# A two-layer hybrid trunk on one core: sliding-window queries kept as [feature, token], their rotation done through memory from GpSimd's queue

## The chip, the cores and the metric

One Trainium2 chip; the kernel runs on 1 of its cores. The metric is device time in microseconds. A core has five engines with queues of their own: PE (TensorE; PEld is its weight load), DVE (VectorE), ACT (ScalarE), POOL (GpSimd) and SP (SyncE, which here issues the transfers).

## The reference, cut to what matters

512 tokens, model width 1024, two layers, float32. Each layer normalises its input, makes one combined projection, runs two branches on it (a gated delta rule with 8 heads, and sliding-window attention with 16 query heads and 2 key/value heads), merges them by gates, projects, and then runs an MLP.

```python
h = rmsnorm(x, pre_mix_g)
proj = h @ w_in        # dn q k v z | beta | decay | sw q | sw k | sw v | gate a | gate b
q = partial_rope(q_in.reshape(B, S, 16, 64), positions)   # rotates the first 16 of 64
k = partial_rope(k_in.reshape(B, S, 2, 64), positions)
scores = einsum(q_block, k_window) * 64 ** -0.5           # window 128, blocks of 128
m = max(max(scores), sink)
probs = exp(scores - m) / (sum(exp(scores - m)) + exp(sink - m))
o = probs @ v
mix = (sigmoid(gate_a) * (dn_out @ w_up_dn) + sigmoid(gate_b) * (o @ w_up_sw)) @ w_o
x = x + rmsnorm(mix, post_mix_g)
x = x + rmsnorm(relu(rmsnorm(x, pre_mlp_g) @ w_ff1) ** 2 @ w_ff2, post_mlp_g)
```

## The kernel before, in words

**Matmuls.** Every large product is three matmuls in a rounded 32-bit format: weights and activations are split into a high and a low part, and high x high, high x low and low x high are summed. Weights come in chunks of 128 x 1024 (512 KB) in the order that `chunk_order` lists. SP loads a chunk, ScalarE copies its high part (`wh`, L319), VectorE subtracts the low part (`wl`, L320), four chunks ahead of use (`LOOK`). There are two forms. In a "unit" (`mm_a`, L335 to L337) the weights stand still and 512 tokens stream: the result is [128 features, 512 tokens], 24 matmuls of 512 columns. `mm_a2` (L346 to L348) is half a unit, 256 tokens. In the other form (`mm_b`, L355 to L357; `mm_b4`, L382 to L384) a tile of 128 tokens stands still and weight columns stream: the result is [128 tokens, columns].

**The norm and its transposes.** The input is [token, feature]; `norm_turn` transposes a token tile on TensorE (`ps_n`, L455) and splits it (ACT L459, DVE L461). In the first layer this is mixed with the first projection by a fixed order. At the layers' turn, `last_tiles` makes the four token tiles of the MLP's last product; the next layer's input tiles 0 and 1 are transposed inside it, tiles 2 and 3 (L555, L558) inside the next layer's first projection.

**The projection of attention queries, keys, values, beta and decay** (1296 columns) is of the second form, in three column blocks of 432 (`NB`): block 0 at L511 to L545 or L551 to L558, blocks 1 and 2 at L655 to L659. `evac_b` copies them to `qt[t]` (queries of a token tile, [token, feature]), `kv[t]` and `ba` (beta and decay). From `ba` a chain of small operations (L605 to L625) leads to a prefix sum on TensorE (`ps_g`, L627) and its transposition (`ps_gt`, L636). This is stored to memory (`gd`), and eight decay masks D are loaded back, cut by GpSimd (L647), raised to powers by ScalarE and stored (`dd`).

**Attention groups between units.** `MIX` (L46) lists 16 steps: which units run (K: a delta-rule key, `ps_kp`; G: gate b, `ps_gb`; A: gate a, `ps_ga`), and after each step's units one attention group (token tile t, key head g, parity e). The first group of a tile rotates queries and keys on GpSimd (`att_rope`, L780 to L785), transposes keys (`ps_k`, L801); each pair of groups transposes four 128 x 128 blocks of queries (`ps_q`, L814), which ScalarE and VectorE scale and split into `qT` (L819, L820). Then come the scores (`ps_s`, L846 and L847), softmax on VectorE and ScalarE (M, L849 to L870), its transposes (`ps_pt`, L876) and the product with the values (`ps_o`, L892), added back into `qt`. After all groups the output is split for the next product (`oT`, L1118 to L1124, 32 pieces of 128 x 128 a layer).

**What sets the order.** The code states the work; a scheduler places each engine's instructions in its queue, free to interleave work that doesn't depend on each other, and keeps to the stated order only inside the `Order` blocks. Each queue then runs strictly in its order.

## Time and profile before

| what | value |
|---|---|
| time, median of 3 runs | 1878.31 us (1876.77 to 1879.1) |
| profiled execution, its own time | 1874.57 us |
| its span, first to last instruction | 1872.9 us |
| mean granted TensorE clock | 0.999 |
| DMA, share of 16 engines, and rate | 42.0% (SP's queue), 136 GB/s |

The profile is of one execution. Its views name an instruction by engine, line, and `out<-in`, the tiles that it writes and reads, with buffer numbers left out. A group's row has its count, then busy time and the mean of one in ns, then idle time of the engine before it and what ended that. A row of the time-ordered view has its start and its length in us, and in brackets the idle time before it. The length of a matmul is modelled and overlaps the next one's, so the distance between starts tells the pace. A row of the windows has a stretch, its length, and the busy time of each engine in it.

### The profile page before, as it was taken

To read this page: it belongs to the slowest core of one execution; us is meant where nothing else is said; L and a number is where in the kernel's file an instruction comes from. 1 tells how busy PE (TensorE), PEld (TensorE's weight loads), DVE (VectorE), ACT (ScalarE), POOL (GpSimd) and SP (SyncE) were. 2 spreads that over 40 slices of the span, in tenths; PEclk is the share of its full clock that TensorE was granted. 3 is DMA by queue.
4 is the path that set the end of the run, shared out by engine and by line. 5 is a ranking of instruction groups with operands and counts; after the bars stand their busy time and mean duration, and the time that the engine had idled before them with its cause. 6 is when DMAs were issued, how large, how long until landed. Compare 5 with 4: busy or idle time off the path is not lost. (4 is left out here: it accounts for less than half of the span.)

```text
span 1872.9 us, 26807 instructions
## 1 busy us (share of the span) xinstructions
PE 1847.6 (99%) x9716; PEld 1534.1 (82%) x9716; DVE 1281.5 (68%) x2466; ACT 939.7 (50%) x1913; POOL 208.1 (11%) x385
## 2 busy tenths in 40 slices
PE   8999999999999999999999999999999999999998
PEld 7888788888888888888888887888888888888886
DVE  5499795777656667684556997857775667586834
ACT  6678732344434645454356887233333346454442
POOL 1322102121100000000012221022111000000000
PEclk9999999999999999999999999999999999999999
DMA  5633436333363253544245333553433533534631
GB/s 179 202 115 117 120 125 196 102 119 109 86 215 127 91 188 97 176 168 170 83 143 188 103 126 105 160 173 102 125 97 110 194 124 99 183 114 158 205 119 45
DMA packets 123445, 255.40 MB, mean 136 GB/s; under 512 B 32609, under 2 KB 49313, under 8 KB 123314
## 3 DMA queue, kind: packets, MB, share of 16 engines
q1 hardware_dynamic: 123314, 253.71, 42.0%
q8 instruction: 76, 1.25, 0.3%
q14 instruction: 55, 0.45, 0.1%
HBM read 224.70 MB, written 28.97 MB: 135 GB/s over the span
## 5 line engine op out<-in xcount | busy, mean ns | idle before, releaser
L320 DVE TENSOR_TENSOR wl<-wr,wh 128x1024 fp32r<-128x1024 f32 (+1 forms) x332 | 402.6, 1222 | 331.2 <-ACT wh L319 323.4
L319 ACT CAST wh<-wr 128x1024 fp32r<-128x1024 f32 (+1 forms) x332 | 344.1, 1041 | 561.8 <-PE ps_f L336 145.9
L335 PE MATMUL ps_f<-g_h,wh 128*128 128x512 f32 x448 | 174.3, 389 | 0.0
L336 PE MATMUL ps_f<-g_l,wh 128*128 128x512 f32 x448 | 174.3, 389 | 0.0
L337 PE MATMUL ps_f<-g_h,wl 128*128 128x512 f32 x448 | 174.3, 389 | 0.0
L397 PE MATMUL ps_p<-wl,P_h 128*128 128x512 f32 x336 | 131.2, 391 | 0.8 <-DVE wl L320 0.8
L399 PE MATMUL ps_p<-wh,P_l 128*128 128x512 f32 x336 | 130.8, 389 | 0.0
L395 PE MATMUL ps_p<-wh,P_h 128*128 128x512 f32 x336 | 129.5, 389 | 0.0
L434 POOL TENSOR_TENSOR pr<-pq,pw 128x1 f32<-128x1 f32 x16 | 9.3, 583 | 809.5 <-DVE pq L433 809.5
L336 PEld LDWEIGHTS ps_f<-g_l,wh 128*128 128x128 f32 x448 | 84.1, 188 | 17.5
L335 PEld LDWEIGHTS ps_f<-g_h,wh 128*128 128x128 f32 x448 | 84.1, 188 | 17.4
L337 PEld LDWEIGHTS ps_f<-g_h,wl 128*128 128x128 f32 x448 | 84.1, 188 | 17.4
L397 PEld LDWEIGHTS ps_p<-wl,P_h 128*128 128x128 f32 x336 | 63.1, 188 | 15.6 <-DVE wl L320 2.3
L395 PEld LDWEIGHTS ps_p<-wh,P_h 128*128 128x128 f32 x336 | 63.1, 188 | 13.3 <-ACT wh L319 0.2
L399 PEld LDWEIGHTS ps_p<-wh,P_l 128*128 128x128 f32 x336 | 63.1, 188 | 12.8
L382 PE MATMUL ps_b<-wh,h_h 128*128 128x432 f32 (+1 forms) x192 | 71.1, 371 | 0.0
L383 PE MATMUL ps_b<-wl,h_h 128*128 128x432 f32 (+1 forms) x192 | 70.4, 367 | 0.0
L384 PE MATMUL ps_b<-wh,h_l 128*128 128x432 f32 (+1 forms) x192 | 70.0, 366 | 0.0
L285 DVE TENSOR_TENSOR wr<-wr 128x1024 f32<-128x1024 f32 x48 | 58.0, 1221 | 2.4 <-DMA wr<-in_weights_dram 1.9
L335 PE MATMUL ps_qp<-h_h,wh 128*128 128x512 f32 x128 | 54.9, 429 | 0.0
L336 PE MATMUL ps_qp<-h_l,wh 128*128 128x512 f32 x128 | 54.1, 423 | 0.0
L864 ACT ACTIVATE M<-M,nm 128x128 f32<-128x128 f32 x128 | 49.8, 391 | 5.9 <-DVE nm L859 5.9
(356 smaller groups left out, 4855.4 us busy)
## 6 DMA issues: line engine op xcount, KB each, us to landing
wr<-in_weights_dram SPq DMA_DIRECT2D x308, 512.0 KB
wr<-in_weights_dram SPq DMA_DIRECT2D x24, 432.0 KB
D<-dd SPq DMA_DIRECT2D x32, 256.0 KB
xd<-xo SPq DMA_DIRECT2D x12, 512.0 KB
xt<-xd SPq DMA_DIRECT2D x24, 256.0 KB
D<-gd SPq DMA_DIRECT2D x16, 256.0 KB
dd<-D SPq DMA_DIRECT2D x16, 256.0 KB
kkd<-kk SPq DMA_DIRECT2D x16, 256.0 KB
```

What stands on the lines that cost most here:

```text
L285: tt(out=a, in0=a, in1=o, op=ALU.add)
L319: nc.scalar.copy(wh[:, :w], wr[:, :w])
L320: sub(out=wl[:, :w], in0=wr[:, :w], in1=wh[:, :w].bitcast(F32), op=ALU.subtract)
L335: mm(ps, lhsT=wh[:, k, :], rhs=hi, start=k == 0, stop=False)
L336: mm(ps, lhsT=wh[:, k, :], rhs=lo, start=False, stop=False)
L337: mm(ps, lhsT=wl[:, k, :], rhs=hi, start=False, stop=k == KT - 1)
L382: mm(pss[t], lhsT=hi[:, tsl], rhs=wh[:, r, :], start=k == 0, stop=False)
L383: mm(pss[t], lhsT=hi[:, tsl], rhs=wl[:, r, :], start=False, stop=False)
L384: mm(pss[t], lhsT=lo[:, tsl], rhs=wh[:, r, :], start=False, stop=k == KT - 1)
L395: mm(pss[t], lhsT=hi[:, c], rhs=wh[:, r, :], start=first, stop=False, skip_group_check=onto)
L397: mm(pss[t], lhsT=hi[:, c], rhs=wl[:, r, :], start=False, stop=False, skip_group_check=onto)
L399: mm(pss[t], lhsT=lo[:, c], rhs=wh[:, r, :], start=False, stop=last, skip_group_check=onto)
```

## The change

Queries are made by eight units of the first form (Q units, `ps_q`), so that they leave the projection as [feature, token] in `q8[g]` and need no transposes. The 272 columns that are left (beta, decay, keys, values) are one block of the second form, in three chunks of 3, 3 and 2 rows. The weights' columns are packed so that the four heads of a unit's rows that rotate stand together.

The rotation of queries needs rows of one head beside their partner rows. It goes through memory: four transfers out of `q8[g]` (`qd`), three in (`rq`), two multiplications and an addition on VectorE with tables of cosine and sine in [feature, token] form, one transfer out (`qrd`) and four back. All twelve are issued from GpSimd's queue. The tables are made once, behind the second Q unit of the first layer, by 16 small copies on ScalarE and eight transposes on TensorE, and kept in memory.

In the first layer, Q unit 0 runs in two token halves around the projection of the last token tile. At the layers' turn, four Q units run in token halves (`halves`, the code that the MLP's first units had), with the transposes of input tiles 2 and 3 inside; the 272-column block follows. The remaining four Q units are in `MIX`, which is listed anew, and the groups come in another order: (0,0), (1,0), (0,1), (1,1) and so on, by tile and key head. A group's preparation (keys' rotation and transposition, `qT`) is stated one group ahead. The decay masks are in a function `decays`, called between Q units 2 and 3 in the first layer. The attention output replaces the queries in `q8`, and is split in pieces of 512 columns. Buffers of 4 KB a partition (`X4`, six) become buffers of 8 KB (`X8`, three).

```diff
-NB = 432
+NB = 272
-MIX = "G K K G K K G K K G K K G GA GA GA".split()
+MIX = "QQ KQ QK G KG KG G KG K GK GK G A A A A".split()
-NA2 = NA + 2
+NA2 = NA + 1
...
+    def halves(aT, name, turn):
+        us = []
+        for i in range(4):
+            us.append(((PZ, PZ, PM, PM)[i](name), weights()))
+            if i != 2:
+                mm_a2(us[i][0], aT, 0, us[i][1])
+                continue
+            for j in range(2):
+                mm_a2(us[i][0], aT, 0, us[i][1], range(j * 4, j * 4 + 4))
+                turn(2 + j)
+        for ps, w in us:
+            mm_a2(ps, aT, 1, w)
+        return [ps for ps, w in us]
...
+        def q_rope(g):
+            spots = [(q8[g][e * HD + a * HALF:e * HD + (a + 1) * HALF].rearrange("p (m n) -> p m n", m=4),
+                      lambda d, a=a, e=e: d[g, a].rearrange("(m e) i n -> e i m n", e=2)[e])
+                     for e in range(2) for a in range(2)]
+            for a, d in spots:
+                pdma(d(qd), a)
+            r_, rs_ = T[2]("rq"), T[3]("rq")
+            flat = lambda d: d.rearrange("a b i n -> (a b i) n")
+            pdma(r_, flat(qd[g]))
+            for a in range(2):
+                pdma(rs_[a * 64:(a + 1) * 64], qd[g, 1 - a].rearrange("b i n -> (b i) n"))
+            tt(out=r_, in0=r_, in1=tables[0][0], op=ALU.mult)
+            tt(out=rs_, in0=rs_, in1=tables[0][1], op=ALU.mult)
+            tt(out=r_, in0=r_, in1=rs_, op=ALU.add)
+            pdma(flat(qrd[g]), r_)
+            for a, d in spots:
+                pdma(a, d(qrd))
+        def q_unit(m, ps=None):
+            if ps is None:
+                ps = PM("ps_q")
+                mm_a(ps, hT)
+            nc.scalar.copy(q8[m // 4][:, m % 4 * 512:(m % 4 + 1) * 512], ps)
+            if m % 4 == 3:
+                q_rope(m // 4)
...
-            ws = [weights() for _ in range(4)]
+            q_tables()
+            ps_q = halves(hT, "ps_q", lambda t: norm_turn(xs_next[t], t, nxt[1]))
+            order.end()
+            for m, ps in enumerate(ps_q):
+                q_unit(m, ps)
+            ws = [weights() for _ in range(3)]
+            pb0 = four(0)
+            for j, w in enumerate(ws):
+                for t in range(NT):
+                    mm_b(pb0[t][:, :NB], ws, hT, t, range(3 * j, min(3 * j + 3, KT)), 3)
...
         def att_q(t, g):
-            ps = PS("ps_q")
-            for i in range(4):
-                j = g * 4 + i
-                tr(ps[:, i * P:(i + 1) * P], qt[t][:, j * P:(j + 1) * P], ident)
+            q_ = c4(q8[g])[:, :, t * P:(t + 1) * P]
...
+        if l == 0:
+            q_unit(0, ps_q0)
+            q_unit(1)
+            rotary()
+            q_tables()
+            q_unit(2)
+            decays()
+            q_unit(3)
+        else:
+            decays()
+        def att_ready(i):
+            if i + 1 < 16 and groups[i + 1][1:] == (0, 0):
+                att_rope(groups[i + 1][0])
+            if i < 16:
+                t, g, e = groups[i]
+                if (g, e) == (0, 0):
+                    att_keys(t)
+                if e == 0:
+                    att_q(t, g)
+        def o_split(g):
+            for i in range(4):
+                oT.append(pair(T[i], "oT"))
+                split(q8[g][:, i * 512:(i + 1) * 512], *oT[-1])
```

Three places in the queues. First GpSimd's in the first layer, from the cut of the decay masks (D) on; `qt` and `kv` are queries and keys of a token tile, `cs` the cosine and sine, `rt` a scratch tile. Before:

```order
L647 AFFINE_SELECT D<-D 128x512 x8
L780 TENSOR_TENSOR rt<-qt_409,cs 128x128
L781 TENSOR_TENSOR rt<-qt_409,cs 128x128
L782 TENSOR_TENSOR rt<-qt_409,cs 128x128
L783 TENSOR_TENSOR rt<-qt_409,cs 128x128
L784 TENSOR_TENSOR qt_409<-rt 128x16x8
L785 TENSOR_TENSOR qt_409<-rt 128x16x8
```

Now, with `q_116` the first half of the queries and `ub` a tile of the delta rule's solver:

```order
L735 AFFINE_SELECT D<-D 128x512 x4
L570 DMA qd<-q_116 8x4x512
L735 AFFINE_SELECT D<-D 128x512 x3
L570 DMA qd<-q_116 8x4x512
L735 AFFINE_SELECT D<-D 128x512
L570 DMA qd<-q_116 8x4x512 x2
L575 DMA rq<-qd 64x512
L821 MEMSET ub 128x1024
L822 MEMSET ub 128x32
L573 DMA rq<-qd 128x512
L575 DMA rq<-qd 64x512
L579 DMA qrd<-rq 128x512
```

The masks were one block, followed by the rotation of queries; now the transfers of the rotation stand between the masks, and no arithmetic on queries is left on GpSimd. Second, the same queue in the second layer, now:

```order
L570 DMA qd<-q_9080 8x4x512 x4
L575 DMA rq<-qd 64x512
L859 TENSOR_TENSOR rt<-kv,cs 128x16
L860 TENSOR_TENSOR rt<-kv,cs 128x16
L861 TENSOR_TENSOR rt<-kv,cs 128x16
L862 TENSOR_TENSOR rt<-kv,cs 128x16
L863 TENSOR_TENSOR kv<-rt 128x2x8
L864 TENSOR_TENSOR kv<-rt 128x2x8
L573 DMA rq<-qd 128x512
L575 DMA rq<-qd 64x512
```

The rotation of the first key tile came to stand between the loads of the queries' rows. Third, TensorE at the layers' turn, around the transposes of input tile 3 (`ps_n`). Before:

```order
L357 MATMUL ps_b<-wh,h_l 128x432
L455 MATMUL ps_n<-ident,xs 128x128 x8
L355 MATMUL ps_b<-wh,h_h 128x432
L356 MATMUL ps_b<-wl,h_h 128x432
L357 MATMUL ps_b<-wh,h_l 128x432
```

Now:

```order
L385 MATMUL ps_q<-h_h,wl 128x256
L506 MATMUL ps_n<-ident,xs 128x128 x8
L383 MATMUL ps_q<-h_h,wh 128x256
L384 MATMUL ps_q<-h_l,wh 128x256
L385 MATMUL ps_q<-h_h,wl 128x256
```

The matmuls around the transposes were those of the 432-column block, with a token tile standing still; now they are halves of Q units.

More of the change, by code (lines that the diff above doesn't have):

```diff
@@ L245, in rotary @@
         act(out=cs[:, :, 0, :], in_=ang, func=AF.Sin, bias=hp, scale=-1.0)
+        for c in range(2):
+            ct = T[6 + c]("ct")
+            cv = ct.rearrange("p (t a b i) -> p t a b i", t=NT, a=2, i=HALF)
+            for a in range(2):
+                for t in range(NT):
+                    src = cs[:, t, c, :].unsqueeze(1).broadcast_to([P, 8, HALF])
+                    act(out=cv[:, t, a], in_=src, func=AF.Copy, scale=-1.0 if c > a else 1.0)
+            ps = PS("ps_cs")
+            for t in range(NT):
+                tr(ps[:, t * P:(t + 1) * P], ct[:, t * P:(t + 1) * P], ident)
+            ctT = T[6 + c]("ctT")
+            nc.scalar.copy(ctT, ps)
+            dma(csd[c], ctT)
     xd = dr.tile([S, D], F32, name="xd")
+    csd = dr.tile([2, P, S], F32, name="csd")
+    qd = dr.tile([2, 2, 8, HALF, S], F32, name="qd")
+    qrd = dr.tile([2, 2, 8, HALF, S], F32, name="qrd")
     gad = dr.tile([KT, P, 512], F32, name="gad")
@@ L893, in att_group @@
                    stop=i == len(pvs) - 1)
-            o_ = qt[t][e * HD:(e + 1) * HD, g * 512:(g + 1) * 512]
-            nc.scalar.copy(o_, po[HD:P])
-            tt(out=o_, in0=po[0:HD], in1=o_, op=ALU.add)
+            o_ = c4(q8[g])[e * HD:(e + 1) * HD, :, t * P:(t + 1) * P]
+            nc.scalar.copy(o_, c4(po[HD:P]))
+            tt(out=o_, in0=c4(po[0:HD]), in1=o_, op=ALU.add)
         inv = []
         sol = solve()
-        n_ = {"K": 0, "G": 0, "A": 0}
-        kind = {"K": k_unit, "G": gb_unit, "A": ga_early}
-        groups = [(t, g, e) for t in range(NT) for g in range(2) for e in range(2)]
+        n_ = {"Q": 4, "K": 0, "G": 0, "A": 0}
+        kind = {"Q": q_unit, "K": k_unit, "G": gb_unit, "A": ga_early}
+        groups = [(t, g, e) for t, g in ((0, 0), (1, 0), (0, 1), (1, 1), (2, 0), (2, 1), (3, 0), (3, 1))
+                  for e in range(2)]
         def fin(g):
@@ L1182, in hybrid_trunk @@
             mT.append(p_)
[L1185 removed]
+        gb1, gb2 = two(X8("gb"))
+        gain(gb1, post_mix_g[l])
+        gb2 = halves_of(gain(gb2, pre_mlp_g[l]))
         q2, h2 = quads("g")
@@ L1309, in hybrid_trunk @@
                 tt(out=acc[t][1], in0=pb_[t], in1=acc[t][1], op=ALU.add)
-        gb3 = gain(post_mlp_g[l])
+        gb3, gb4 = two(X8("gb"))
+        gain(gb3, post_mlp_g[l])
+        xos = [a for i in range(2) for a in two(X8("xo"))]
         h3 = []
```

273 lines of the change are left out of this document (130 added, 143 removed).

## The prediction

> **What bounds the kernel now.** I read the page first: busy shares and granted clock.
>
> ```profile
> span 1872.9 us, 26807 instructions
> PE 1847.6 (99%) x9716; PEld 1534.1 (82%) x9716; DVE 1281.5 (68%) x2466; ACT 939.7 (50%) x1913; POOL 208.1 (11%) x385
> PEclk9999999999999999999999999999999999999999
> ```
>
> TensorE is busy nearly the whole span, at the granted clock's top step. So the time is the number of matmuls times the pace at which they start, plus TensorE's few waits. The view of TensorE's waits shows how few:
>
> ```profile
> PE ps_n L455 <- DVE xs L446: 5.5, 7, 2.2
> PE ps_pt L876 <- ACT M L870: 3.9, 6, 0.8
> PE ps_g L627 <- DVE lw L625: 1.0, 1, 1.0
> ```
>
> The norm's transposes wait for VectorE (kernel start and layers' turn), softmax's transposes for ScalarE's last scaling, the decay's prefix sum for VectorE. That is 10.4 us of 1873. In the stage that the change rebuilds (K and gate units with attention groups between) TensorE is not alone:
>
> ```profile
> 100.00:150.00 50.00, 48.98 (x263) 40.26 (x262) 46.43 (x134) 40.13 (x117) 13.82 (x22) 1.00 0.33 101
> 150.00:200.00 50.00, 49.62 (x261) 40.57 (x261) 44.98 (x140) 38.82 (x115) 15.12 (x28) 1.00 0.43 125
> ```
>
> The columns are PE, PEld, DVE, ACT, POOL, clock, DMA share. VectorE is at 46.43 of 50 us, so a gain of TensorE alone could be eaten there (a rival, below).
>
> **The change, part by part.** The profiled execution took 1874.57 us: its span of 1872.9 and 1.67 around it. The median of the runs shown is 1878.31, so 3.74 above it. I sum changes against the profiled execution and carry the same difference to the median.
>
> *Matmul pace.* A matmul's shown length is modelled and overlaps its neighbour, so I price by starts. From the time-ordered view, three stretches without a wait: 512, 432 and 256 columns.
>
> ```profile
> 913.97 0.39 PE L382 MATMUL ps_b<-wh,h_h 128*128 128x512 f32 x1
> ...
> 916.24 0.39 PE L383 MATMUL ps_b<-wl,h_h 128*128 128x512 f32 x1
> ```
>
> ```profile
> 956.13 0.35 PE L357 MATMUL ps_b<-wh,h_l 128*128 128x432 f32 x1
> ...
> 961.77 0.35 PE L356 MATMUL ps_b<-wl,h_h 128*128 128x432 f32 x1
> ```
>
> ```profile
> 612.69 0.28 PE L348 MATMUL ps_f<-g_h,wl 128*128 128x256 f32 x1
> ...
> 614.24 0.28 PE L346 MATMUL ps_f<-g_h,wh 128*128 128x256 f32 x1
> ```
>
> They span 10, 29 and 13 starts: 2.27/10 = 0.227 us, 5.64/29 = 0.1945, 1.55/13 = 0.1192. No row shows 272 columns; on the straight line from 256 to 432 it is 0.1192 + 16 x (0.1945 - 0.1192)/176 = 0.126 (bounds: 0.119, and 0.1192 x 272/256 = 0.127).
>
> *Projection of queries, keys, values, beta, decay.* Before: 3 column blocks x 4 token tiles x 24 = 288 matmuls of 432 a layer, 576 x 0.1945 = 112.0 us. After: 96 of 272 and 8 query units of 24 matmuls a layer, 192 x 0.126 + 384 x 0.227 = 111.4. So -0.6. Five of the units (one in the first layer, four in the second) run in token halves: 240 x 0.1192 instead of 120 x 0.227, +1.4.
>
> *Query transposes.* Queries now leave the projection as [feature, token], so the 64 transposes go:
>
> ```profile
> L814 PE MATMUL ps_q<-ident,qt 128*128 128x128 f32 x64 | 9.6, 272 | 0.0
> ```
>
> ```profile
> 131.64 0.60 PE L814 MATMUL ps_q<-ident,qt 128*128 128x128 f32 x4
> 132.00 0.48 PE L337 MATMUL ps_kp<-h_h,wl 128*128 128x512 f32 x1
> 132.31 0.39 PE L335 MATMUL ps_kp<-h_h,wh 128*128 128x512 f32 x1
> ```
>
> From the first of four transposes to the second 512-column start lie 0.67 us, of which one 512-column matmul is 0.227: 0.44 for a group of four. 16 groups: -7.1. Eight transposes of the new cosine and sine tables come in, 2 x 0.44 = +0.9. TensorE's work: -0.6 + 1.4 - 7.1 + 0.9 = -5.4 us.
>
> *The wait of the prefix sum* in the first layer:
>
> ```profile
> 36.56 0.17 DVE L592 COPY ba<-ps_b 128x16 f32<-128x16 f32 x1
> ```
>
> ```profile
> 40.40 0.35 PE L383 MATMUL ps_b<-wl,h_h 128*128 128x432 f32 x1
> 41.78 0.38 PE L627 MATMUL ps_g<-lw,le 128*128 128x32 f32 x2 [1.03 <-DVE lw L625]
> ```
>
> 1.38 us between starts where 0.19 is the pace: 1.2 lost. The chain takes 5.2 us from the last copy of beta (36.56). After, half a query unit (2.9), a unit (5.4) and part of another stand between the last projection tile and this matmul, so it should be gone: -1.2 (bounds: 0, if the table work put on ScalarE there delays the chain, and -1.2).
>
> *The layers' turn.* The last two token tiles of the second layer's input arrive late; TensorE works on what it has:
>
> ```profile
> 949.24 0.96 PE L455 MATMUL ps_n<-ident,xs 128*128 128x128 f32 x5 [0.85 <-DVE xs L446]
> ```
>
> ```profile
> 952.53 0.35 PE L357 MATMUL ps_b<-wh,h_l 128*128 128x432 f32 x1
> 954.61 1.29 PE L455 MATMUL ps_n<-ident,xs 128*128 128x128 f32 x8 [1.73 <-DVE xs L446]
> ```
>
> Tile 3 comes at 954.61 whatever TensorE does. By then it had done 48 matmuls of 432, 48 x 0.1945 = 9.3 us of useful work; now 72 halves, 72 x 0.1192 = 8.6. The rest is done later: +0.7.
>
> ```profile
> 955.90 1.36 DVE L461 TENSOR_TENSOR h_l<-ps_n,h_h 128x512 fp32r<-128x512 f32 x2 [0.17 <-ACT h_h L459]
> ```
>
> Tile 3 was split by 957.26, 2.65 us after its transposes began; behind them now stand 24 halves of the fourth unit (2.9 us) before anything reads tile 3, so nothing new is late there.
>
> *The rotation through memory.* This is the new wait. Queries now go to memory, back as rows, through three VectorE operations, to memory and back into place: four transfers in a row, 12 issues for each of 4 chains, all in GpSimd's queue, which in the kernel before issues none. Two waiting places stand in that queue with them. In the first layer, the decay masks (eight selects on D) come between the issues:
>
> ```profile
> 47.73 3.33 POOL L647 TENSOR_SCALAR_AFFINE_SELECT D<-D 128x512 f32<-128x512 f32 x4 [28.97 <-DMA D<-gd]
> ...
> 57.91 0.63 POOL L647 TENSOR_SCALAR_AFFINE_SELECT D<-D 128x512 f32<-128x512 f32 x1 [1.45 <-DMA D<-gd]
> ```
>
> In the second, the keys' rotation stands between two of its loads and waits for the projection's evacuation:
>
> ```profile
> 75.07 0.27 POOL L780 TENSOR_TENSOR rt<-kv,cs 128x16 f32<-128x16 f32 x1
> ...
> 77.16 0.21 POOL L785 TENSOR_TENSOR kv<-rt 128x16 f32<-128x16 f32 x1
> ```
>
> Hops of memory that this kernel shows, from issue to landing, on the chain of waits, are the shortest and the longest:
>
> ```profile
> 1414.61 2.73 DMA fd<-ff
> ...
> 1445.59 5.52 DMA fb<-fd
> ```
>
> and the engine work behind them, as groups (the last two rows are the preparation of a group of queries):
>
> ```profile
> L1052 DVE TENSOR_TENSOR yf<-yf,fb 128x512 f32<-128x512 f32 x16 | 11.0, 686 | 16.1 <-DMA fb<-fd 16.1
> L820 DVE SCALAR_TENSOR_TENSOR qT<-ps_q,qT 64x512 fp32r<-64x512 f32 x32 | 22.0, 689 | 1.8 <-ACT qT L819 0.9
> L819 ACT ACTIVATE qT<-ps_q 64x512 fp32r<-64x512 f32 x32 | 18.9, 591 | 6.8 <-DVE qT L820 5.2 <-PE ps_q L814 1.3
> ```
>
> ```profile
> 13.72 0.71 PE L355 MATMUL ps_b<-wh,h_h 128*128 128x432 f32 x1
> ```
>
> ```profile
> 960.82 0.51 ACT L593 COPY qt<-ps_b 128x416 f32<-128x416 f32 x1 [2.94 <-DVE ba L592]
> ```
>
> First layer: the last select ended at 58.5; four hops of 2.73 to 5.52, three operations of 0.69, then 0.59 + 0.69: ready between 72.7 and 83.9. TensorE reaches the first scores after the fourth query unit (about 52: from the first projection matmul at 13.7 some 12 us of projection, 22 of query units and 4 of transposes and the slower first starts) and six more units of 24 x 0.227 plus 2.5: about 87. Not late. Second layer: from the evacuation of the first key tile TensorE has the rest of that projection (2.1), four units (21.8) and a little, 24.3 us, to the first scores. The chain has 0.5 for the evacuation, 2.3 for the keys' rotation, three hops (8.2 to 16.6), 2.1, one select (0.6), 1.3: 15.0 to 23.4, and on top whatever five issues cost GpSimd, which no row shows. At nothing the slack is 0.9 to 9.3; at 1 us each (an estimate, a little over one of GpSimd's selects, 3.33/4 = 0.83) it is -4.1 to 4.3. I take 1 us late in this place, none in the other three (the chains of the second four units have some 39 us): +1.0, bounds 0 and 16 (each of four chains 4 us late). The weights' transfers stay in SP's queue and are not behind this; there the change adds two stores and four loads of 256 KB for the tables, which I put at nothing beside 332 weight loads.
>
> By the Trainium skill's page "DMA: Bandwidth & Descriptors", section "Anatomy of one DMA — SWDGE (gpsimd) path", a transfer issued from GpSimd takes about 2.0 us plus its bytes at 436 GB/s, so (estimate by that page) 2.6 us for 256 KB, no chain would be late, and the sum would be better by the 1.0. The trace speaks against so short a time: even 2 KB (fd<-ff) took 2.73.
>
> *Work at no cost.* The 64 small splits of the attention's output shown here become 16 of 512 columns:
>
> ```profile
> L407 DVE TENSOR_TENSOR oT_l<-qt,oT_h 128x128 fp32r<-128x128 f32 x64 | 16.7, 298 | 4.9 <-ACT qq L665 2.9 <-ACT oT_h L406 1.5 <-PE ps_k L801 0.5
> ```
>
> VectorE: -16.7 + 16 x 0.69 = -5.7, and +8.2 for the rotation (12 x 0.69); the queries' rotation leaves GpSimd. Hidden, as TensorE did not wait there. Groups prepared one ahead shorten no listed wait: softmax's transposes waited for M, not for queries. I keep the 3.9 us.
>
> Sum: -5.4 - 1.2 + 0.7 + 1.0 = **-4.9**: 1869.7 for a profiled execution, 1873.4 for the median. About 0.2% (3.8 us) is what a measurement of this kernel tells from no change.
>
> **Rivals.**
>
> *The chains in GpSimd's queue come late* (the other side). If an issue holds GpSimd for 2 us instead of 1, the second layer's first scores are 5 us later, and the other chains, with 12 issues each, use up their slack. At 3 us each for four chains it is 12 in place of my 1: 1884.4. The point from which it decides: 1 + 4.9 + 3.8 = 9.7 us of waits. For it: VectorE waited 16.1 us in 16 times at L1052 for the last hop of a chain of four, so such chains land about 1 us later than the order of the work allows for. Against: 35 us of TensorE work stand between. The Trainium skill's page "SBUF — State Buffer", section "Who interferes with whom", gives the same outcome a cause: GpSimd's descriptors can't be written while VectorE is in a two-port mode. By that page the forms that hold VectorE here (tensor_tensor, tensor_reduce, scalar operations on PSUM) mostly don't enter it, so I add little to the chance. 0.20.
>
> *VectorE bounds the attention stage*, and TensorE's 7.1 us of transposes turn into waiting: 1873.4 + 7.1 = 1880.5. For it: 46.43 of 50. Against: TensorE is at 48.98 and 49.62 there, and the first K units now run ahead of the first group, in a stretch where VectorE has room:
>
> ```profile
> 45.00:70.00 25.00, 25.00 (x131) 24.23 (x130) 6.68 (x6) 17.66 (x51) 5.67 (x8) 1.00 0.89 286
> ```
>
> 6.68 of 25 us. 0.18.
>
> *The softmax waits go too*, for that last reason, and no chain is late: 1873.4 - 1.0 - 3.9 = 1868.5. 0.12.
>
> **How the numbers follow.** Forecast 0.50, its own range 1870 to 1877 (prefix sum 0 to -1.2, chains 0 to 4, softmax 0 to -3). The range to the other cases is 1867 to 1884: it leaves out most of the first rival's upper half and a little at the bottom. Faster by over 0.2% (under 1874.5): two thirds of the forecast and the last rival, 0.46. Slower (over 1882.1): nearly all of the first rival, 0.18. The same: 0.36.
>
> **What would show it.** In the changed profile: no ps_q transposes; ps_g without a wait; at the turn, a wait before tile 3's transposes about 0.7 us longer in work; TensorE's waits for M as before; first scores (ps_s) of the second layer waiting about 1 us for qT. The forecast is wrong if scores, or softmax behind them, wait several us after each rotation, if DVE stands for rq, or if TensorE's total work does not fall by 5 us.

## The result, and the profile after

The change made the kernel slower: 1906.99 us median (1902.71 to 1909.84), against 1877.54 for the kernel before in the same series; the ratio is 1.0156, 95% interval 1.0133 to 1.0179. That is +29 us where -5 was forecast. The profiled execution took 1902.71 us, the fastest of the four; its span is 1901.0, 28.1 more than the span before. The page of the changed kernel:

```profile
span 1901.0 us, 26868 instructions
PE 1853.7 (98%) x9780; PEld 1528.0 (80%) x9780; DVE 1289.3 (68%) x2420; ACT 942.9 (50%) x1882; POOL 214.3 (11%) x385
```

The shares of busy time are as before, within two points; nothing in these two lines tells of the loss. The view of TensorE's waits does (total us, times, longest):

```profile
PE ps_n L506 <- DVE xs L497: 6.4, 7, 2.8
PE ps_us L372 <- DVE tmp L833: 5.5, 2, 2.8
PE ps_pt L948 <- ACT M L940: 3.9, 6, 1.2
PE ps_s L916 <- DVE qT L898: 3.4, 4, 1.9
PE ps_kp L372 <- ACT sgb L799: 2.9, 2, 1.5
...
PE ps_o L964 <- ACT pf_h L458: 2.3, 7, 0.9
PE ps_o L964 <- POOL pc L958: 2.3, 2, 1.1
PE ps_ud L373 <- DVE yT_l L459: 2.1, 1, 2.1
PE ps_a L771 <- DVE kk L754: 1.8, 1, 1.8
PE ps_gb L372 <- ACT q L587: 1.5, 1, 1.5
```

Of the three waits that the prediction quoted, two are there near their old totals (norm 5.5, now 6.4; softmax 3.9, now 3.9, its longest 1.2 in place of 0.8), and that of the prefix sum is gone. All other lines shown are new or several times what they were, and they lie in the two attention stages, save yT_l. The same stage by windows, from the first scores to the first ps_us: the kernel before (two layers), then the changed kernel (two layers). Columns are PE, PEld, DVE, ACT, POOL, granted clock, DMA share, GB/s:

```profile
84.12:249.10 164.98, 162.08 (x832) 131.48 (x831) 142.18 (x418) 127.09 (x377) 36.83 (x59) 1.00 0.35 109
1012.44:1177.44 165.00, 162.10 (x833) 131.50 (x831) 141.98 (x416) 127.11 (x377) 36.85 (x59) 1.00 0.35 110
```

```profile
91.61:262.41 170.80, 161.66 (x802) 128.81 (x803) 146.26 (x397) 127.22 (x354) 35.80 (x53) 1.00 0.38 117
1013.64:1206.33 192.69, 179.94 (x867) 144.12 (x868) 149.73 (x399) 140.59 (x396) 41.32 (x64) 0.97 0.41 126
```

First minus second number of a row is TensorE's idle time: 2.90 and 2.90 before, 9.14 and 12.75 after. The windows do not hold equal work (the matmuls are in brackets), so idle times compare only roughly. Over the stage VectorE and ScalarE are not full in either kernel (146.26 of 170.80). And the second layer's clock is at 0.97. Stretch by stretch, in windows of 3 and 4 us, the changed kernel's clock behind its waits:

```profile
258.00:261.00 3.00, 1.67 (x8) 1.05 (x6) 3.00 (x6) 1.90 (x3) 0.00 (x0) 1.00 0.35 138
261.00:264.00 3.00, 1.59 (x7) 1.37 (x8) 3.00 (x11) 0.78 (x2) 0.00 (x0) 1.00 0.02 5
264.00:267.00 3.00, 3.00 (x15) 2.49 (x14) 3.00 (x12) 0.63 (x1) 0.00 (x0) 1.00 0.00 0
...
1011.00:1014.00 3.00, 1.06 (x7) 0.60 (x6) 2.42 (x5) 1.76 (x3) 1.89 (x3) 1.00 1.03 240
1014.00:1017.00 3.00, 3.00 (x14) 2.50 (x14) 2.83 (x6) 2.97 (x13) 2.18 (x7) 0.65 0.64 186
1017.00:1020.00 3.00, 3.00 (x12) 2.41 (x11) 0.00 (x0) 3.00 (x13) 0.00 (x0) 0.78 0.79 306
...
1034.00:1038.00 4.00, 2.28 (x8) 1.76 (x9) 3.61 (x11) 3.83 (x8) 2.43 (x4) 0.68 0.06 7
1038.00:1042.00 4.00, 4.00 (x13) 3.23 (x12) 3.81 (x8) 1.84 (x4) 1.42 (x3) 0.50 0.85 178
...
1206.00:1209.00 3.00, 2.67 (x6) 2.15 (x7) 3.00 (x13) 0.63 (x1) 0.00 (x0) 0.51 0.00 0
```

Behind the wait of 1.94 us for qT the clock fell to half for 3.4 us, behind the string of waits around 1031 for 6.8, and at the wait of 2.77 at 1206 for 3.4. The wait of 2.74 at 262 was followed by none (the last section says why). The kernel before has no such stretch between its first 20 and its last 5 us.

The whole account, from the start of every matmul against the start before it plus the paces of the prediction: a step over its pace by more than 0.24 us (0.1 for short matmuls) is put down as a wait, one over by 0.12 to 0.24 as the half clock (a 512-column step is 0.427 there), the rest as small delays. Up to the last matmul's start:

| us | before | after | difference |
|---|---|---|---|
| matmuls at their pace | 1797.2 | 1792.0 | -5.2 |
| waits, first attention stage | 4.6 | 11.5 | +6.9 |
| waits, second attention stage | 4.4 | 16.0 | +11.6 |
| waits elsewhere | 21.4 | 29.2 | +7.8 |
| steps at half clock | 3.9 | 7.3 | +3.4 |
| small delays | 34.1 | 37.3 | +3.2 |
| sum | 1865.6 | 1893.3 | +27.7 |

The row of the half clock counts only steps of that excess. The clock record of the changed kernel's trace has 13.7 us at half clock between its first 20 and its last 5 us, which can cost at most 6.8; so a part of the clock's cost stands in the other rows.

Elsewhere: 2.0 between the prefix sum and the first layer's first scores, 2.1 for the second layer's first qT, 3.0 behind the second layer's solve (2.1 of it for yT_l), the rest small. In the second layer the loss begins here, on ScalarE (time-ordered view):

```profile
1012.24 0.63 ACT L897 ACTIVATE qT<-q 64x512 fp32r<-64x512 f32 x1 [2.02 <-DMA q<-qrd]
...
1015.91 3.60 ACT L739 ACTIVATE D<-D,ngc 128x128 f32<-128x128 f32 x12
1019.42 0.39 ACT L737 ACTIVATE egl<-D 128x4 f32<-128x4 f32 x3
1019.72 3.61 ACT L739 ACTIVATE D<-D,ngc 128x128 f32<-128x128 f32 x12
1023.35 0.63 ACT L897 ACTIVATE qT<-q 64x512 fp32r<-64x512 f32 x1
...
1025.66 0.62 ACT L753 ACTIVATE th<-kk 128x512 f32<-128x512 f32 x1
```

```profile
1030.01 0.71 PE L771 MATMUL ps_a<-kk 128*128 128x128 f32 x4 [1.83 <-DVE kk L754]
```

The decay's exponentials (L739), 0.3 us each, fill ScalarE from 1014.4 to 1023.3 with 28 of their 32, between the first scores and their softmax; the key unit's tanh (L753) and TensorE's ps_a wait behind them. They are there because the block of beta and decay now comes after four query units in the second layer. The rotation has a part in it too: in ScalarE's queue these 28 stand behind the first row's qT, which waited 2.02 us for the last transfer of the rotated queries.

### The profile page after: what moved, and what is told of

Read it like the earlier page. It is cut to its first block, busy times and chain, and to the rows that moved or that the text cites. A ratio compares the mean times of both kernels' runs of the same rounds, so it can differ in the third digit from the quotient of the medians.

```text
span 1901.0 us, 26868 instructions
## 1 busy us (share of the span) xinstructions
PE 1853.7 (98%) x9780; PEld 1528.0 (80%) x9780; DVE 1289.3 (68%) x2420; ACT 942.9 (50%) x1882; POOL 214.3 (11%) x385
## 4 chain that ended last, share of the span: by engine, by line
PE 59%; DVE 6%; DMA 3%; ACT 3%; issue 2%; POOL 1%; SPq 0%; DVEq 0%; POOLq 0%; ACTq 0%
PE ps_f L373 5%; PE ps_f L372 5%; PE ps_f L374 5%; PE ps_p L434 3%; PE ps_p L436 3%; PE ps_p L432 3%; PE ps_b L421 2%; PE ps_b L419 2%; PE ps_b L420 2%; DVE wl L357 1%; PE ps_ud L373 1%; DMA fb<-fd 1%; PE ps_ud L374 1%; PE ps_ud L372 1%; DMA wr<-in_weights_dram 1%
## 5 line engine op out<-in xcount | busy, mean ns | idle before, releaser
L436 PEld LDWEIGHTS ps_p<-wh,P_l 128*128 128x128 f32 x336 | 63.1, 188 | 12.8
L372 PE MATMUL ps_us<-oT_h,wh 128*128 128x512 f32 x128 | 50.7, 396 | 5.5 <-DVE tmp L833 5.5
L372 PE MATMUL ps_kp<-h_h,wh 128*128 128x512 f32 x128 | 50.9, 397 | 2.9 <-ACT sgb L799 2.9
L372 PE MATMUL ps_gb<-h_h,wh 128*128 128x512 f32 x128 | 52.0, 406 | 1.5 <-ACT q L587 1.5
```

The source lines that it names most:

```text
L372: mm(ps, lhsT=wh[:, k, :], rhs=hi, start=k == 0, stop=False)
L436: mm(pss[t], lhsT=lo[:, c], rhs=wh[:, r, :], start=False, stop=last, skip_group_check=onto)
```

## The experiments

Three theories at the start. **1:** the queries' round trip in GpSimd's queue. **2:** the decay's exponentials, late in the second layer. **3:** the new order of attention groups and units. A fourth came of the first eight runs: the stage is paced by ScalarE and VectorE, so TensorE's savings there are worth nothing (balance); against it, a fifth: the static order of the in-order queues decides, and any edit makes it anew (order). Each run was timed beside the kernel before; the changed kernel's ratio to compare with is 1.0156. Most intervals reach about 3 us to either side, so a difference of 3 or 4 us between two runs is not clear of noise. "Idle" is TensorE's time without work in the two stages, from windows as above, in us.

**e1, rotation's loads left out:**

```diff
             for a, d in spots:
                 pdma(d(qd), a)
-            r_, rs_ = T[2]("rq"), T[3]("rq")
+            return
```

> Leaves out part of the computation: the queries are stored to memory by GpSimd's four issues per chain, but nothing is loaded back, so they are not rotated (eight of twelve issues and three VectorE operations per chain are gone). Changed kernel: 1907. Theory 1 (the round trip in GpSimd's queue costs the second layer its 12.7 us of stalls between 1000 and 1050, with the clock's drop, and the first layer 1 to 2): 1891 to 1895. Theory 2 (not the chain, but the decay's exponentials, which now come after four query units in the second layer and stand on ScalarE in front of the first softmax): only the wait for qT of 2.1 us and the 1.4 us of slow clock behind it go, 1902 to 1905. Theory 3 (the new order of attention groups and units costs 7 us in each layer, the chains nothing): 1904 to 1907.

It took 1903.28 us, ratio 1.0141 (1.0125 to 1.0156); idle 8.64 and 13.11. Theory 1 falls as the main cause: with no rotated queries to wait for, the kernel is 3.7 us faster, which is inside the intervals. The first scores came 25 us earlier in the first layer (66.47), and the stage's end hardly moved (260.69, was 262.41).

**e2, only the last hop left out:**

```diff
             pdma(flat(qrd[g]), r_)
-            for a, d in spots:
-                pdma(a, d(qrd))
```

> Leaves out part of the computation: the rotated queries are stored to memory but not loaded back into place, so the scores use unrotated ones. GpSimd's queue keeps the waits for the first landing and for VectorE, eight issues per chain; TensorE and ScalarE no longer wait for the last hop. If the cost is that queries come late (theory 1a): as without the loads, 1891 to 1895. If it is what stands behind the issues in GpSimd's queue (theory 1b: masks of the decay, keys' rotation, second halves of the probabilities): 1900 to 1905. Theories 2 and 3: 1903 to 1907.

It took 1898.16 us, ratio 1.0114 (1.0099 to 1.0129); idle 12.10 and 13.30. Less was left out than in e1, and by the medians more was gained, though these two intervals just overlap. The time lies between those of 1a and 1b, and neither explains why e1 gains less; it was the first sign that an edit's number is not the price of what it takes away.

**e3, the second layer's block first** (with the token tiles at the turn as in the kernel before):

```diff
-        for c in ("BQQQQ" if l == 0 else "QQQQB") + "".join(MIX):
+        for c in "BQQQQ" + "".join(MIX):
...
-            ps_q = halves(hT, "ps_q", lambda t: norm_turn(xs_next[t], t, nxt[1]))
+            for t in range(NT):
+                mm_b(pb0[t][:, :NB], ws, hT, t, range(4), 3)
```

> The second layer's block of beta, decay, keys and values goes first again, ahead of its four query units (as in the first layer), with the turn's transposes between its token tiles as in the kernel before. Computes the same. At the turn TensorE has 6 us of work where it had 8.6, so +2.5 there. Theory 2 (late decay exponentials): the second layer's stalls of 12.7 us fall to 3 to 5, in all 1897 to 1903. Theory 1 (the round trip): the fourth query unit is now nearer to the first scores, stalls stay or grow, 1907 to 1912. Theory 3: 1908 to 1910.

It took 1898.59 us, ratio 1.0112 (1.0097 to 1.0127); idle 8.57 and 8.61. The second layer's stage now idles like the first's, as theory 2 has it. The edit also runs that layer's query units whole, not in token halves.

**e4, preparation not ahead:**

```diff
+            if i:
+                att_ready(i)
             g = att_group(*groups[i])
...
-            att_ready(i + 1)
```

> The preparation of a group (query scaling and split, key transposes, the keys' rotation) is asked for directly ahead of its group instead of one group earlier. Computes the same. Theory 3 in this form (preparing ahead pushes ScalarE's and VectorE's softmax work back): the waits for M, sgb, pf_h and pc shrink by half, 1898 to 1902. Theories 1 and 2: 1905 to 1912, since queries and keys then come later still.

It took 1905.04 us, ratio 1.0150 (1.0129 to 1.0171); idle 9.90 and 12.29. The intervals overlap; preparing ahead shows neither as the cause nor as a gain.

**e5, small splits of the attention's output:**

```diff
-                split(q8[g][:, i * 512:(i + 1) * 512], *oT[-1])
+                    q_ = q8[j // 4][:, j % 4 * 512 + t * P:j % 4 * 512 + (t + 1) * P]
+                    split(q_, hi[:, tsl], lo[:, tsl])
```

> The attention's output is split again in 32 pieces of 128 columns per layer, by token tile, as in the kernel before; all else as changed. Computes the same. Theory (the four 512-column splits of the second half come in one burst on VectorE, after the last group, in front of the convolution's reads of ps_vp, and hold the first ps_us 2.9 us in each layer): both waits go, and the slow clock behind the second, 1899 to 1901. If the wait only moves to the other work on VectorE and ScalarE at that place: 1905 to 1908.

It took 1902.52 us, ratio 1.0135 (1.0120 to 1.0151); idle 7.95 and 12.07. The place is real. In the changed kernel's VectorE the four wide splits stand in front of the convolution's reads of ps_vp, and ps_us waits for that buffer. VectorE's rows come first, then TensorE's, whose bracket names what ended on VectorE last (tmp):

```profile
257.17 3.12 DVE L459 TENSOR_TENSOR oT_l<-q,oT_h 128x512 fp32r<-128x512 f32 x4
...
261.53 0.74 DVE L750 SCALAR_TENSOR_TENSOR vv<-ps_vp,cw,vv 128x511 f32<-128x511 f32 x1
```

```profile
262.41 0.47 PE L372 MATMUL ps_us<-oT_h,wh 128*128 128x512 f32 x1 [2.74 <-DVE tmp L833]
```

With small splits these waits fell from 5.5 to 2.5 us in all, while a wait of 1.5 came at ps_zp and those of the scores for qT grew from 3.4 to 6.3. So the waits moved, and the 4.5 us of the medians are inside the intervals.

**e6, list of units and group order of before:**

```diff
-MIX = "QQ KQ QK G KG KG G KG K GK GK G A A A A".split()
+MIX = "QQQQG K K G K K G K K G K K G GA GA GA".split()
-NA2 = NA + 1
+NA2 = NA + 2
```

with the groups by token tile again.

> The units' list, the group order and the number of early gate units as in the kernel before, with the four later query units ahead of them; all else as changed. Computes the same. Theory 3 (the order of groups and units makes the stalls of 1 to 2 us in the attention stage, some 5 us a layer): 1895 to 1899. Theory 1 (the chains): the second half of the queries is now wanted at the third group instead of the fifth, so more waiting for qT, 1908 to 1917.

It took 1891.20 us, ratio 1.0074 (1.0057 to 1.0091): 16 us better, more than theory 3 asked; idle 6.82 and 11.78. Its profiled execution was the slowest of its four (1898.56; the others 1889.95 to 1892.33), so the trace shows little of the gain. The queries wanted earlier cost nothing to speak of (1.3 us of waits for qT).

**e7, block first and loads left out** (e1's and e3's diffs together):

> Two earlier edits at once: the second layer's block of beta, decay, keys and values first, and the queries' rotation left out (stored, not loaded back). If the late decay masks and the round trip each hide behind the other: the second layer's stalls of 12.7 us fall to 2 to 4, 1889 to 1893. If they are one cause, already gone with the block first: as that run, 1898. If they are separate and add, 8 and 4 us: 1894 to 1896.

It took 1895.68 us, ratio 1.0104 (1.0089 to 1.0120); idle 9.14 and 7.68. That is 2.9 better than e3, inside the intervals.

**e8, three edits back** (the diffs of e3, e5 and e6 together):

> Three edits at once: block of beta, decay, keys and values first in the second layer, small splits of the attention's output, and the units' list and group order of the kernel before. Queries as [feature, token], their rotation in GpSimd's queue and the preparation one ahead stay. Computes the same. If the three causes are separate and these are they: 1884 to 1889. If the chains are what is left, with the later queries wanted at the third group: 1893 to 1903.

It took 1895.07 us, ratio 1.0096 (1.0081 to 1.0111); idle 6.52 and 7.88. One by one the three gave 8, 4 and 16 us; together they gave 12, no more than e6 alone. That the three causes are separate and add up has fallen.

**e9, the kernel before without its query transposes:**

```diff
-            ps = PS("ps_q")
-            for i in range(4):
-                j = g * 4 + i
-                tr(ps[:, i * P:(i + 1) * P], qt[t][:, j * P:(j + 1) * P], ident)
+            ps = qt[t][:, g * 512:(g + 1) * 512]
```

> The kernel before, with the 64 query transposes left out: the scaling and splitting of a group's queries reads the untransposed queries instead, as many operations on as many elements, so the scores are of wrong numbers. If TensorE's time bounds the attention stage there, as the prediction took it: 7 us less than before, 1870. If the stage is paced by the softmax chain on ScalarE and VectorE (theory 4), the time saved turns into waiting: 1874 to 1877.

It took 1889.22 us, ratio 1.0065 (1.0052 to 1.0079): 12 us *slower*, with 7 us less work for TensorE. Neither theory allowed for that. Reading the queries from another place is not the reason: ScalarE's scaling takes 0.63 us in place of 0.59, 1.2 us over all 32. The stages' windows, both layers:

```profile
88.63:258.67 170.04, 163.86 (x804) 132.46 (x804) 141.51 (x416) 126.77 (x376) 39.13 (x59) 0.97 0.35 107
1025.54:1193.85 168.31, 161.21 (x803) 130.08 (x804) 141.24 (x414) 126.79 (x376) 39.12 (x59) 0.99 0.35 108
```

Idle is 6.18 and 7.10, and the clock record has 17.1 us at half clock, which can cost 8.5. How it begins, on ScalarE, then TensorE:

```profile
82.38 0.63 ACT L816 ACTIVATE qT<-qt 64x512 fp32r<-64x512 f32 x1 [3.46 <-POOL qt L785]
...
86.47 0.24 ACT L806 CAST kT_h<-ps_k 64x128 fp32r<-64x128 f32 x1
```

```profile
88.63 0.47 PE L843 MATMUL ps_s<-kT_h,qT 128*128 128x128 f32 x1 [2.73 <-ACT kT_h L806]
```

The scaling of the next queries (qT), no longer behind a transpose of TensorE, stands earlier in ScalarE's queue, waits 3.46 us for GpSimd's rotation, and holds the key copy (kT_h) that the first scores need. In the kernel before, kT_h comes here on ScalarE, and these scores do not wait:

```profile
81.33 0.24 ACT L806 CAST kT_h<-ps_k 64x128 fp32r<-64x128 f32 x1
```

**e10, transposes put into the changed kernel:**

```diff
+            ps = PS("ps_x")
+            for i in range(4):
+                tr(ps[:, i * P:(i + 1) * P], q_[:, i], ident)
```

> The changed kernel with 64 more transposes on TensorE, four with each preparation of a pair of groups as in the kernel before; nothing reads what they write, so it computes the same. If TensorE's time bounds the stage: +7, 1914. If the softmax chain paces it (theory 4): 1906 to 1909, the transposes run inside the waits, and since they keep TensorE busier perhaps a little less.

It took 1909.28 us, ratio 1.0175 (1.0161 to 1.0189); idle 8.53 and 9.24. The 7 us of TensorE's time cost 2.3, inside the intervals, as if TensorE had time to spare there in the changed kernel.

**e11, the second layer's exponentials left out,** and the stores of their masks:

```diff
-                for c in range(NC):
+                for c in range(NC if l == 0 else 0):
```

> Leaves out part of the computation: in the second layer the 32 exponentials of the decay masks on ScalarE and the 8 stores of the masks; the selects on GpSimd and the 8 small exponentials stay. Theory 2 (these exponentials, 0.3 us each and 10 us in all, come after four query units and stand in ScalarE's queue in front of the first softmax and the key units): the second layer's stalls between 1000 and 1050 fall from 12.7 to 4, 1897 to 1900. If the masks on GpSimd or the rotation's transfers do it: 1904 to 1907.

It took 1896.30 us, ratio 1.0106 (1.0092 to 1.0120); idle 9.25 and 8.13. The second stage, to compare with the changed kernel's:

```profile
1018.36:1203.19 184.83, 176.70 (x868) 141.43 (x868) 149.73 (x399) 132.75 (x368) 35.75 (x59) 0.99 0.39 119
```

ScalarE has 7.84 us less to do there, TensorE idles 4.62 less, and the clock is at 0.99; the stage is 7.9 us shorter, and the kernel 10.7. Two different edits, e3 and this one, thus bear out theory 2 as a part of the second layer's loss.

**e12, more gate units between the groups** (e8, and):

```diff
-MIX = "QQQQG K K G K K G K K G K K G GA GA GA".split()
+MIX = "QQQQG K K G K K GA K K G K KA G GA GA GA".split()
-NA2 = NA + 2
+NA2 = NA
```

> As the run with three edits back (block of beta, decay, keys and values first, small splits, the units' list and group order of before), and two more gate units of 24 matmuls run between the attention groups, taken from behind the output projection. Computes the same. If the softmax chain paces the stage and TensorE has time to spare there (theory 4): 11 us a layer of gate units cost only half or less, 1878 to 1886. If TensorE is what is scarce: as that run, 1893 to 1897.

It took 1904.60 us, ratio 1.0153 (1.0138 to 1.0168); idle 6.91 and 9.31. That is 9.5 us worse than e8, of which 3.5 are two waits outside the stage that e8 does not have (ps_qk, for a load of kk). The time to spare that e10 suggested is not there for the taking; balance alone has fallen too.

**e13, the kernel before with one transpose instead of four:**

```diff
-            for i in range(4):
+            tr(ps[:, 0:P], qt[t][:, g * 512:g * 512 + P], ident)
```

> The kernel before, with one query transpose instead of four for each pair of groups; the scaling and splitting reads its 128 columns four times, as many elements as before, so the scores are of wrong numbers. The preparation stays tied to TensorE and 48 transposes (5.3 us) are gone. Order (the tie is what held the stage together): 1871 to 1874. Balance (ScalarE and VectorE pace the stage): 1877 to 1881, or up to 1889 as without any transposes if the waits bring the half clock.

It took 1883.17 us, ratio 1.0030 (1.0018 to 1.0042); idle 6.76 and 6.63, clock 1.00. It is not faster either, so holding the preparation back by a transpose (the tie) is not all that makes the kernel before good; but the half clock does not come, and it is 5 us worse and not 12.

**e14, the kernel before with two entries exchanged:**

```diff
-MIX = "G K K G K K G K K G K K G GA GA GA".split()
+MIX = "K G K G K K G K K G K K G GA GA GA".split()
```

> The kernel before with the first entries of the units' list changed from G K K G to K G K G; the same units, the same work, computes the same. If the order of before is a good one among many and any change of it costs waits: 1881 to 1889. If order by itself matters little (balance): 1875 to 1879.

It took 1884.38 us, ratio 1.0039 (1.0024 to 1.0053); idle 4.71 and 4.17. The same units and the same work are 6 us slower, clear of noise: the order of before is better than the one neighbour of it that was tried.

**e15, the changed kernel tied** (one transpose for each pair of groups goes in, and the scaling reads its columns four times, so the scores are of other numbers):

```diff
+            tr(ps[:, 0:P], q_[:, 0], ident)
...
-                act(out=c4(a[rh]), in_=q_[rh], func=AF.Copy, scale=HD ** -0.5)
+                act(out=c4(a[rh]), in_=four_(ps[rh]), func=AF.Copy, scale=HD ** -0.5)
```

> The changed kernel with one transpose for each pair of groups on TensorE, and the scaling and splitting of queries reading that transpose's 128 columns four times (wrong numbers, as many elements): the preparation is tied to TensorE's place again. Order: the stage's waits fall from 11.5 and 16 us towards 5 a layer, 1893 to 1898. Balance: 1905 to 1910.

It took 1886.87 us, ratio 1.0048 (1.0031 to 1.0065): 20 us better than the changed kernel, the most of any edit. The stages:

```profile
98.56:258.15 159.59, 154.71 (x777) 123.95 (x776) 135.02 (x373) 121.81 (x347) 31.41 (x52) 1.00 0.37 114
1024.55:1195.97 171.42, 165.72 (x828) 133.50 (x826) 142.88 (x394) 125.53 (x351) 32.48 (x54) 0.99 0.39 120
```

Idle is 4.88 and 5.70. The two profiled executions, the fastest of four there and the slowest here, lie only 12.8 us apart. All of the change is in it but the preparation's freedom from TensorE.

**e16, three edits back, not ahead, and tied** (the diffs of e8, e4 and e15 together):

> The version with three edits undone (block first, small splits, list and group order of before), preparation not ahead, and the same tie (wrong numbers, as many elements). What is left of the change is the projection of queries by units, the rotation in GpSimd's queue and the tables. Order: 1878 to 1884. Balance: 1893 to 1897.

It took 1903.02 us, ratio 1.0138 (1.0123 to 1.0153); idle 12.18 and 11.73. Every edit in it had helped alone or done nothing, and together they are 16 us worse than e15. TensorE waited 8.9 us for two ps_zp buffers (VectorE's convolution, L751).

**e17 and e18, the changed kernel with two entries exchanged** (the same work):

```diff
-MIX = "QQ KQ QK G KG KG G KG K GK GK G A A A A".split()
+MIX = "QQ KQ QK G KG KG G KG GK K GK G A A A A".split()    (e17)
+MIX = "QQ KQ QK KG G KG G KG K GK GK G A A A A".split()    (e18)
```

> The changed kernel with the ninth and tenth entries of its units' list exchanged (K, GK to GK, K): the same units, the same work, computes the same. If any new order moves the attention stages by several us: 4 to 15 us away from 1907, either way, with other waits in the attention stage than 11.5 and 16 us. If the tie's 20 us are its own: 1904 to 1910.

> The changed kernel with the fourth and fifth entries of its units' list exchanged (G, KG to KG, G): the same units, the same work, computes the same. As the run beside it: 4 to 15 us away from 1907 either way if any new order moves the stages, 1904 to 1910 if not.

They took 1902.86 us, ratio 1.0140 (1.0124 to 1.0155), and 1902.00, ratio 1.0134 (1.0117 to 1.0151); idle 8.94 and 12.30, and 6.99 and 10.23. By the medians, exchanges that change no work move this kernel by 4 and 5 us, at the edge of what was expected and inside the intervals; only the 6 us of e14 are clear of them. So the numbers of e1, e4, e5, e7 (beside e3) and e10 are no prices. What is beyond that: undoing the late exponentials (8 to 11 us better), the list and group order (16) or the free preparation (20), and taking the transposes from the kernel before (12 worse). Since the first three do not add up, they are no shares of the loss either.

## Why the prediction was wrong, step by step

**TensorE's work, -5.4:** right, -5.2. The 272-column step that no row had shown is 0.127 (96 of them from 977.0 to 989.2); 0.126 was taken.

**The prefix sum, -1.2:** the wait went, and one of the table's transposes now waits for ScalarE one microsecond later. TensorE's time-ordered view:

```profile
42.36 0.38 PE L713 MATMUL ps_g<-lw,le 128*128 128x32 f32 x2
...
44.98 0.33 PE L274 MATMUL ps_cs<-ident,ct 128*128 128x128 f32 x1 [0.92 <-ACT ct L271]
```

The step costs 1.17 over pace there, so the net is nothing: the upper of the bounds given, by the table work that it named, though in another place.

**The layers' turn, +0.7:** right in kind. The two waits are 0.60 and 2.18 us, in place of 0.85 and 1.73: +0.2 together.

**The chains, +1.0 and the first rival, +11:** the second layer was late as forecast, by a little more. Its first scores waited 1.94 us for qT. The first layer, called "Not late", was late as well: its first scores waited 0.71 us for qT at 91.61, though they came 4.6 later than the 87 that was worked out. An issue holds GpSimd about 0.55 us (1 was taken), and the hops were longer than the rows of before: 6.1 and 7.0 us for the last two in that place. GpSimd's queue there:

```profile
978.90 2.24 POOL L570 DMA_DIRECT2D qd<-q  x4 [18.36 <-ACT q L587]
984.32 0.56 POOL L575 DMA_DIRECT2D rq<-qd  x1 [3.17 <-issue]
...
989.97 0.61 POOL L573 DMA_DIRECT2D rq<-qd  x1
...
999.41 0.58 POOL L579 DMA_DIRECT2D qrd<-rq  x1 [7.12 <-DVE rq L578]
...
1005.82 2.22 POOL L581 DMA_DIRECT2D q<-qrd  x4 [1.34 <-DMA qrd<-rq]
```

In all, e1 and e7 put the chains at 3 to 4 us, which these runs can't tell from the exchanges, and e2 puts the last hop alone at 9. The first rival's 1884.4 is the nearest of the times that the prediction named, still 23 short, and e1 speaks against it as the main cause. The Trainium skill's 2.0 us plus bytes ("DMA: Bandwidth & Descriptors", section "Anatomy of one DMA — SWDGE (gpsimd) path") gives 2.6 us for 256 KB (an estimate by that page). Three of the four such stores agree (2.3, 2.3 and 2.9), so the prediction set it aside too lightly; the one in that place took 6.1.

**Work at no cost:** this is the step that failed. It said "Hidden, as TensorE did not wait there" of VectorE's and ScalarE's work, "I keep the 3.9 us" of the softmax waits, and the sum then took TensorE's 7.1 us of transposes as time. The 3.9 us did stay, by luck to the digit, since the longest of them is 1.2 in place of 0.8. But a wait that is not in the list of before is not a wait that can't come: every engine works through its queue in a fixed order, and the change made that order anew for all queues of the two stages. 18.5 us of waits came on balance, in some dozen new places of 0.5 to 2.9 us, and the half clock behind them. e9 shows the step failing by itself: the same 7 us of transposes, taken from the kernel before, cost 12.

**VectorE bounds the stage (second rival, 1880.5):** it had the right place and the wrong price. It took the loss as at most the time saved, TensorE waiting instead of transposing. VectorE was not full over the stage (146.26 of 170.80), though it was for some stretches (3.00 of 3.00 us from 258 to 267), and waits behind a queue's head have no such cap.

**Moved work:** that the block of beta and decay comes 21.8 us later at the second layer was counted at the turn and for the rotation, not for its 32 exponentials. Those 9.8 us of ScalarE had stood in a stretch without any softmax, where VectorE was busy for 1.06 of 11.68 us (979.45 to 991.13 in the kernel before), and most of them landed on the first softmax: 8 to 11 us (e3, e11), the largest single part that the runs can price with its mechanism. Since they stood behind the wait for the rotated queries, this price and that of the last hop (e2) may be in part the same.

**Open:** why tying the preparation helps the changed kernel by 20 us and its repaired version not at all; the runs show that a new order alone can cost several us (e14), not a rule for a good one, and that order is the whole of the loss is argued. The number of buffers (three of 8 KB in place of six of 4 KB) was not varied by itself. A run with the order of before held fixed while only the transposes go was not tried, since the order is written out anew with every edit. No version here beats the kernel before; of the changed ones that leave nothing out, e6 comes nearest, 14 us behind.

## What to carry to other kernels

Where an order for in-order engines is made from estimates, price a change by what it takes off the busiest engine only if the order of the other queues stays; else put the cost of a new order, here up to 6 us for an exchange without any work and 12 for less work, into the range on the slow side. Before forecasting a gain in a stage where VectorE stands at 86% and ScalarE at 77%, look at what ties an operation to its place: a transpose on TensorE also holds back the copy that reads it. When a block is moved, follow all that it feeds, and look for whom its work on the other engines now stands in front.

## What the runs showed of the hardware

TensorE's clock fell to 0.50 behind waits of only about 2 us, or behind several of 0.5 to 2 us within 7, for 3.4 or 6.8 us at a time; other waits as long (2.74 at 262, 2.18 at 961) left it at 1.00, and so did the 1.73 of the kernel before. The clock records of the traces show what tells them apart. In all 17 runs in which the clock fell in mid-run, it did so on a grid of 3.413 us: the three falls of the changed kernel, at 1014.93, 1035.41 and 1206.07, lie 6 and 50 such steps apart. Over all 20 traces, without the first 25 and the last 12 us, a step at full clock in which TensorE stood idle for 1.9 us or more in all was followed by half clock in 42 of 42 cases, one with 1.5 to 1.9 us in 13 of 41, and one with less in 2 of more than 10,000. The wait of 2.74 at 262 lay across the border of two steps, with 0.9 us of idle time in one and 1.8 in the other, and that at 961 in the same way with 1.1 and 1.2. So it is the idle time within one step that counts, and where the border lies decides whether a wait of 2 us brings the half clock.

The Trainium skill, "TensorE: Matmul & The Clock Gate", section "What's actually happening", has the clock fall after an idle window of about 3.4 us, and says that the window runs freely. The length of the window agrees with these records, but an idle window is not needed: no wait in the changed kernel's trace is longer than 2.8 us.

A step at half clock can cost 1.7 us, so the wait of 1.94 us for qT could cost 3.6. The four executions of the changed kernel fit: spans of 1901.0, 1904.5, 1906.1 and 1908.1 us at mean clocks of 0.996, 0.994, 0.993 and 0.992; 0.004 of 1901 is 7.6 us, and they lie 7.1 apart. Other runs do not follow the clock so closely (e6 took 1892.33 at 0.999 and 1889.95 at 0.997), so it is not the whole of the spread.
